# Batched 64x64 matrix products on one core: the first quarter of the first `a` tile loaded as three transfers of 32, 32 and 64 partitions

## The chip, the cores and the metric

The kernel runs on one core of one Trainium2 chip. A core has a matrix engine (TensorE, PE), VectorE (DVE), ScalarE (ACT), GpSimd (POOL) and SyncE (SP), and sixteen DMA engines which move data between the chip's main memory and the core's own. Each of SyncE, ScalarE and GpSimd can issue transfers, and each of them has a DMA queue of its own. The metric is the device time of one execution in microseconds.

## The reference

```python
def setup_inputs():
    return {
        "a": np.random.randn(1024, 64, 64).astype(np.float32),
        "b": np.random.randn(1024, 64, 64).astype(np.float32),
    }

def reference(a, b):
    return np.matmul(a, b).astype(np.float32)
```

There are 1024 independent products of a 64x64 matrix with a 64x64 matrix, with float32 in and out. Each of the three arrays has 16.8 MB. The kernel multiplies in bf16.

## The kernel before

The 1024 products are cut into 8 pairs of tiles (`s`, 128 products each), and into 16 tiles (`t`, 64 products each). For each `s`, one tile of `a` and one of `b` are loaded, 128 partitions wide, in four quarters (`h`, 32 products each).

**Loads.** Most loads are issued by GpSimd (`load_a`, L83, and `load_pair`, L113): each brings 32 partitions, 512 KB of float32 from main memory, and turns them into 256 KB of bf16 on the way. They go four to an `a` or `b` tile. The first `a` tile alone takes another path (`load_first_a`, L85 to L96): it is loaded as float32, with no conversion, by SyncE (quarters 0 and 2) and ScalarE (quarters 1 and 3), each quarter in one transfer of 128 partitions with 4 KB each, 512 KB in all. In this path a product's 64 rows lie in four partitions with 16 rows each, so a quarter's 32 products fill 128 partitions. The view that is read is this one, where `g` counts the products of a quarter and `mp` the four row blocks of a product:

```python
a_v = a.rearrange("(s g h) (mp v) k -> s h g mp (v k)", h=4, g=32, v=16)
```

The quarters land in two buffers that later serve as output tiles (`o_sb`), two quarters to a buffer.

**Turning the first tile.** `turn_first_a(h)` runs for h = 0 to 3 in this order. It turns quarter h into bf16 (L103: VectorE for h = 0, ScalarE for h = 1, 2 and 3) and transposes it in blocks of 32x32 on VectorE (L104). Each cast waits for the whole of its quarter.

**Spreading, products, evacuation.** `spread` (L142 for the first two tiles, L149 later) copies the transposed `a` into block-diagonal tiles `at_bd`, which are zeroed once (L252 on VectorE, L253 and L257 on GpSimd). `turn` (L121) and `turn_a` (L129) transpose `b` and the later `a` tiles on VectorE. `products` (L195) multiplies on TensorE, and `evacuate` (L207, L213) copies the results from PSUM to an output tile, mostly on ScalarE. `store(t)` sends the output tile out in two halves of 512 KB (L222).

**Order.** The order on each engine is written out by hand at the end of the kernel (L248 to L287). On GpSimd it is: a memset (L253), the four loads of `b` for s = 0, four of `a` for s = 1, four of `b` for s = 1, a memset (L257), `a` and `b` for s = 2, and from then on the stores with the loads of later tiles between them. GpSimd's transfers use eight semaphores in turn, so the ninth is issued only after the first has landed: eight are in flight at most. The four stores of the last tile are in pieces of 256 KB, three on SyncE and one on ScalarE. SyncE has nothing else in its queue than its two quarters of the first `a` tile and these three stores.

Of the kernel before, what the change touches and what calls it, by code (L numbers as in the profile page):

```python
# [12 lines left out]
def kernel(  # L13
# [14 lines left out]
    nc = tc.nc  # L28
# [19 lines left out]
    }  # L48
    LAST_QUEUE = {0: nc.sync, 2: nc.sync, 4: nc.scalar, 6: nc.sync}

    a_v = a.rearrange("(s g h) (mp v) k -> s h g mp (v k)", h=4, g=32, v=16)
    ap_v = a.rearrange("(s g h) m k -> s h g (m k)", h=4, g=32)
    bp_v = b.rearrange("(s g h) k n -> s h g (k n)", h=4, g=32)
# [31 lines left out]
    def load_first_a():  # L85

        raw = [
            o_pool.tile([128, 8, 4, 64], fp32, name="o_sb")[:].rearrange(
                "p gh w n -> p (gh w n)"
            )  # L90
            for _ in range(2)
        ]
        parts = [raw[h % 2][:, 1024 * (h // 2) : 1024 * (h // 2) + 1024] for h in range(4)]
        for h in range(4):
            (nc.scalar if h % 2 else nc.sync).dma_start(out=parts[h], in_=a_v[0, h])
        a_tiles[0] = parts  # L96

    def turn_first_a(h):
# [148 lines left out]

    with tc.manual_schedule():  # L248
        load_first_a()
        nc.vector.memset(warm[:, 0:1], 0.0)  # L250
        nc.scalar.copy(warm[:, 1:2], warm[:, 0:1])  # L251
# [66 lines left out]
```

## Time and profile before

| | us |
|---|---|
| median of 3 runs | 128.21 (127.74 to 128.29) |
| the profiled execution | 128.62 |
| its span, from the first to the last instruction | 126.8 |
| VectorE busy | 102.9 (81%) |
| ScalarE busy | 96.0 (76%) |
| GpSimd busy | 64.9 (51%) |
| TensorE matmuls busy | 54.9 (43%) |
| SyncE's two issues of the first `a` tile | 0.58 and 0.63 |
| issue to landing, SyncE's quarters, median | 5.8 |
| issue to landing, ScalarE's quarters, median | 7.4 |
| issue to landing, GpSimd's loads, median | 9.5 |

The profile shows one execution. Its engines' lines give busy times; in its slices a digit is the busy share of a fortieth of the span in tenths. The DMA lines tell how busy the sixteen DMA engines were and what they moved, counted as written. In the views by time, the first number is the start in microseconds from the beginning of the span and the second the duration; after the instruction, square brackets hold the idle time of the engine before it and what ended that idle time. The letter q behind an engine (SPq) marks its sequencer, which issues transfers.

### The profile page before, as it was taken

The page shows a single profiled execution, that of the slowest core. Times are in us where ns is not written, and L with a number is a line of the kernel's source. Part 1 is how long each engine was busy: PE and PEld are TensorE (multiplying, and loading weights), DVE is VectorE, ACT ScalarE, POOL GpSimd, SP SyncE. Part 2 cuts the span into 40 slices and gives each one's busy share as a digit, 9 for nine tenths or more (in the row PEclk, how much of TensorE's full clock was granted, in tenths as well). Part 3 has the DMA queues.
Part 4 walks back from the last instruction along what each step waited for, and adds up shares of the span by engine and source line. Part 5 has one row for each costly group of instructions (what it writes and reads, how often), then busy time and mean ns, then how long its engine had stood idle before and what let it go on. Part 6 is the DMA issues. An engine that isn't in the chain of part 4 may idle for free.

```text
span 126.8 us, 2680 instructions
## 1 busy us (share of the span) xinstructions
PE 54.9 (43%) x1088; PEld 51.7 (41%) x1088; DVE 102.9 (81%) x93; ACT 96.0 (76%) x151; POOL 64.9 (51%) x96
## 2 busy tenths in 40 slices
PE   0000019028645485847352942047510777079400
PEld 0000019028645484847352932046510776079300
DVE  4956999999999999999969696896949789780810
ACT  2157920399999999999999889918898299999700
POOL 8962797428544655625544446474554464333100
PEclk9999999955586555555955599657755555555965
DMA  2999999999999999999999999999999999999992
GB/s 59 392 327 209 212 217 217 212 215 207 264 293 257 264 290 292 291 292 278 265 275 290 291 288 284 275 275 275 296 288 283 275 273 279 383 406 396 343 342 99
DMA packets 8875, 34.76 MB, mean 274 GB/s; under 512 B 1568, under 2 KB 2592, under 8 KB 6944
## 3 DMA queue, kind: packets, MB, share of 16 engines
q0 software_dynamic: 7200, 31.46, 91.9%
q1 hardware_dynamic: 1104, 1.84, 4.3%
q10 hardware_dynamic: 560, 1.31, 2.7%
q8 instruction: 8, 0.13, 0.4%
q14 instruction: 3, 0.02, 0.0%
HBM read 33.55 MB, written 16.78 MB: 397 GB/s over the span
## 4 chain that ended last, share of the span: by engine, by line
DMA 57%; DVE 15%; ACT 7%; issue 7%; PE 5%; POOL 3%; ACTq 1%; DVEq 0%; POOLq 0%
DMA a_sb<-in_a_dram 28%; DMA b_sb<-in_b_dram 15%; DMA out_dram<-o_sb 7%; DMA o_sb<-in_a_dram 7%; DVE at_sb L129 6%; ACT o_sb L213 4%; PE o_ps L195 3%; DVE b_bf L121 3%; POOL out_dram L222 3%; ACT at_bd L149 2%; DVE o_sb L213 2%; DVE at_bd L142 2%; PE t_ps L195 1%; DVE at_bd L149 1%; ACT a_bf L103 1%
## 5 line engine op out<-in xcount | busy, mean ns | idle before, releaser
L195 PE MATMUL o_ps<-b_bf,at_bd 128*128 128x64 bf16 (+1 forms) x1024 | 52.0, 232 | 63.7 <-ACT o_sb L213 35.7
L195 PEld LDWEIGHTS <-at_bd 128*128 128x128 bf16 (+1 forms) x1088 | 51.7, 127 | 66.8 <-issue 43.0
L213 ACT COPY o_sb<-o_ps 64x512 f32<-64x512 f32 x112 | 65.0, 580 | 7.7 <-PE o_ps L195 6.1
L222 POOL DMA_DIRECT2D out_dram<-o_sb x30 | 23.8, 792 | 31.1 <-DMA a_sb<-in_a_dram 8.4
L121 DVE STREAM_TRANSPOSE b_bf<-b_sb 128x1024 f32<-128x1024 f32 x16 | 34.3, 2195 | 4.9 <-DMA b_sb<-in_b_dram 4.7
L129 DVE STREAM_TRANSPOSE at_sb<-a_sb 128x1024 f32<-128x1024 f32 x14 | 26.2, 1948 | 3.8 <-issue 2.4
L149 DVE COPY at_bd<-at_sb 32x1024 f32<-32x1024 f32 x40 | 28.2, 705 | 1.1
L113 POOL DMA_DIRECT2D b_sb<-in_b_dram x32 | 17.7, 554 | 14.9 <-DMA b_sb<-in_b_dram 6.9
L149 ACT COPY at_bd<-at_sb 32x1024 f32<-32x1024 f32 x16 | 16.7, 1043 | 8.6 <-DVE at_sb L129 8.3
L83 POOL DMA_DIRECT2D a_sb<-in_a_dram x28 | 16.4, 590 | 6.3 <-DMA out_dram<-o_sb 4.7
L103 ACT CAST a_bf<-o_sb 128x1024 bf16<-128x1024 f32 x3 | 3.1, 1045 | 4.7 <-DMA o_sb<-in_a_dram 4.7
L213 DVE COPY o_sb<-t_ps 64x256 f32<-64x256 f32 x8 | 3.4, 422 | 3.9 <-PE t_ps L195 3.8
L104 DVE STREAM_TRANSPOSE at_sb<-a_bf 128x512 f32<-128x512 f32 x4 | 4.2, 1048 | 2.6 <-ACT a_bf L103 2.6
L142 ACT COPY at_bd<-at_sb 32x512 f32<-32x512 f32 x8 | 4.9, 615 | 0.2
L252 DVE MEMSET at_bd<- 128x4096 f32 x1 | 3.5, 3472 | 0.8 <-issue 0.8
L253 POOL MEMSET at_bd<- 128x4096 f32 x1 | 3.5, 3512 | 0.3 <-POOLq L302 0.3
L257 POOL MEMSET at_bd<- 128x4096 f32 x1 | 3.5, 3537 | 0.0
L142 DVE COPY at_bd<-at_sb 32x512 f32<-32x512 f32 x8 | 3.3, 414 | 0.2
L251 ACT ACT_TABLE_LOAD x1 | 1.3, 1283 | 2.3 <-issue 2.3
L195 PE MATMUL t_ps<-b_bf,at_bd 128*128 128x64 bf16 x64 | 3.0, 224 | 0.0
L213 ACT COPY o_sb<-t_ps 64x256 f32<-64x256 f32 x8 | 2.9, 367 | 0.1
L207 ACT COPY o_sb<-o_ps 128x1024 f32<-128x1024 f32 x2 | 1.9, 1015 | 0.1
(7 smaller groups left out, 1.4 us busy)
## 6 DMA issues: line engine op xcount, KB each, us to landing
out_dram<-o_sb POOLq DMA_DIRECT2D x30, 512.0 KB, 9.3
b_sb<-in_b_dram POOLq DMA_DIRECT2D x32, 256.0 KB, 9.5
a_sb<-in_a_dram POOLq DMA_DIRECT2D x28, 256.0 KB, 9.5
o_sb<-in_a_dram ACTq DMA_DIRECT2D x2, 512.0 KB, 7.4
o_sb<-in_a_dram SPq DMA_DIRECT2D x2, 512.0 KB, 5.8
out_dram<-o_sb SPq DMA_DIRECT2D x3, 256.0 KB, 5.4
out_dram<-o_sb ACTq DMA_DIRECT2D x1, 256.0 KB, 5.5
```

Of the source, the lines that this page charges most:

```text
L83: nc.gpsimd.dma_start(out=a_tiles[s][32 * h : 32 * h + 32], in_=ap_v[s, h])
L103: (nc.scalar.copy if h else nc.vector.tensor_copy)(rows, a_tiles[0][h])
L104: nc.vector.transpose(at_tiles[0][:, h].rearrange("p g w mp vo -> p w vo g mp"), rows.bitcast(fp32).rearrange("p (vo w kp) -> p w vo kp", ...
L113: nc.gpsimd.dma_start(out=b_tiles[s][32 * h : 32 * h + 32], in_=bp_v[s, h])
L121: nc.vector.transpose(cols[:, u], rows[:, u])
L129: nc.vector.transpose(cols[:, 2 * half : 2 * half + 2].rearrange("p mp vo w g -> p (mp vo) w g"), rows[:, 2 * half : 2 * half + 2].rearran ...
L142: copy(bd[rows, 8 * i : 8 * i + 8, :, h, :, :].rearrange("p g w mp vo -> p (g w) (mp vo)"), at_sb[block : block + 32, h].rearrange("p g w ...
L149: copy(bd[rows, :, :, h, :, :].rearrange("p g w mp vo -> p (g w) (mp vo)"), at_sb[rows, half].rearrange("p g w mp vo -> p (g w) (mp vo)"),)
L195: nc.tensor.matmul(place, at_bd[:, w, g, :, u], b_bf[:, g, 64 * u : 64 * u + 64], start=u == 0 and (first or not split), stop=u == 1 and ( ...
L213: copy(rows[64 * par : 64 * par + 64, :, :, wl, :], o_ps[64 * wl : 64 * wl + 64, :, par, :, :],)
L222: store_queue(t, lo).dma_start(out=o_v[t, :, lo : lo + n, :], in_=o_sb[:, lo : lo + n].rearrange("p gh w n -> p (gh w n)"),)
L252: nc.vector.memset(bd_tiles[0][:], 0.0)
```

## The change

Quarter 0 of the first `a` tile was one transfer on SyncE. It becomes three on SyncE: products 0 to 8, 8 to 16 and 16 to 32 of the quarter, that is 32, 32 and 64 partitions, with 128, 128 and 256 KB. The other three quarters stay as they are, on the same queues; SyncE's quarter 2 stands behind the three pieces in its queue. The cast of quarter 0 waits for all three. Nothing else in the program changes, on any engine, apart from the numbers of lines, which grow by nine.

```diff
+    FIRST_LOADS = [
+        (0, nc.sync, 0, 8),
+        (0, nc.sync, 8, 16),
+        (0, nc.sync, 16, 32),
+        (1, nc.scalar, 0, 32),
+        (2, nc.sync, 0, 32),
+        (3, nc.scalar, 0, 32),
+    ]
...
-        for h in range(4):
-            (nc.scalar if h % 2 else nc.sync).dma_start(out=parts[h], in_=a_v[0, h])
+        for h, queue, lo, hi in FIRST_LOADS:
+            queue.dma_start(out=parts[h][4 * lo : 4 * hi], in_=a_v[0, h, lo:hi])
         a_tiles[0] = parts
```

## The prediction

> **What bounds the kernel now.** I read the slices first, then the queues, then stretches of one and two microseconds, then the order of time around the first tile.
>
> ```profile
> DMA  2999999999999999999999999999999999999992
> GB/s 59 392 327 209 212 217 217 212 215 207 264 293 257 264 290 292 291 292 278 265 275 290 291 288 284 275 275 275 296 288 283 275 273 279 383 406 396 343 342 99
> DMA packets 8875, 34.76 MB, mean 274 GB/s; under 512 B 1568, under 2 KB 2592, under 8 KB 6944
> ...
> q0 software_dynamic: 7200, 31.46, 91.9%
> q1 hardware_dynamic: 1104, 1.84, 4.3%
> q10 hardware_dynamic: 560, 1.31, 2.7%
> ```
>
> The sixteen DMA engines are busy from the second slice (3.2 us long) to the last but one. The GB/s row changes only with the kind of transfer: GpSimd's loads turn float32 into bf16, so that 256 KB written are 512 KB read. Queue 0 is GpSimd's; queue 1 is SyncE's, with the two quarters of `a` that the change concerns. The same in stretches:
>
> ```profile
> 2.00:3.00 1.00, 0.00 (x0) 0.00 (x0) 1.00 (x1) 0.69 (x1) 1.00 (x1) 1.00 0.83 147
> ...
> 5.00:6.00 1.00, 0.00 (x0) 0.00 (x0) 0.96 (x3) 0.00 (x0) 1.00 (x3) 1.00 1.04 418
> ...
> 7.00:8.00 1.00, 0.00 (x0) 0.00 (x0) 0.57 (x1) 0.39 (x1) 1.00 (x3) 1.00 1.30 459
> 8.00:9.00 1.00, 0.00 (x0) 0.00 (x0) 0.47 (x1) 0.33 (x1) 0.42 (x1) 1.00 0.94 197
> ...
> 33.00:34.00 1.00, 1.00 (x23) 1.00 (x21) 1.00 (x1) 0.99 (x2) 0.20 (x1) 0.50 1.00 385
> ...
> 122.00:124.00 2.00, 0.00 (x0) 0.00 (x0) 0.00 (x0) 0.00 (x0) 0.00 (x0) 0.50 1.03 346
> 124.00:126.80 2.80, 0.00 (x0) 0.00 (x0) 0.00 (x0) 0.00 (x0) 0.00 (x0) 0.50 0.18 62
> ```
>
> The last two numbers are DMA share and GB/s (packets count where they start, so a share may pass 1). Data flow from a little after 2 us; until 8 us it is the first `a` tile at 410 to 460 GB/s, then the rate halves: GpSimd's converting loads, the first issued at 4.19, have taken over. From 3 to 124 us there is no gap. So what the change does to an engine of arithmetic costs nothing unless it starves the DMA engines; what it does to their work or its split counts in full.
>
> ```profile
> 0.73 1.54 ACTq L95 DMA_DIRECT2D o_sb<-in_a_dram  x2
> ...
> 0.74 1.26 SPq L95 DMA_DIRECT2D o_sb<-in_a_dram  x2
> ...
> 5.09 0.79 DVE L103 CAST a_bf<-o_sb 128x1024 bf16<-128x1024 f32 x1
> ...
> 8.67 1.04 ACT L103 CAST a_bf<-o_sb 128x1024 bf16<-128x1024 f32 x1 [1.28 <-DMA o_sb<-in_a_dram]
> ...
> 10.56 1.05 ACT L103 CAST a_bf<-o_sb 128x1024 bf16<-128x1024 f32 x1 [0.84 <-DMA o_sb<-in_a_dram]
> ...
> 27.85 0.79 POOL L222 DMA_DIRECT2D out_dram<-o_sb  x1 [2.92 <-ACT o_sb L213]
> ...
> 33.80 0.79 POOL L222 DMA_DIRECT2D out_dram<-o_sb  x1 [1.08 <-DMA b_sb<-in_b_dram]
> ```
>
> SyncE issues two quarters in 1.26 us. The first has landed when VectorE leaves its memset at 5.09, the third (SyncE's second) at 8.65, the fourth (ScalarE's second) at 10.54. The first store waits for arithmetic that began with that landing. By 33.80 GpSimd is held by transfers again: it may have eight in flight.
>
> **The change part by part.** *Issues.* SyncE's two issues take 583 and 627 ns; there will be four, so the third quarter is issued at 2.55 instead of 1.37, 1.2 us later. Nothing else stands in SyncE's queue until the last stores at 118 us, so the two issues cost nothing themselves. The trace has no issue of 32 partitions; the nearest rows are these and the final stores' 373 to 489 ns, which bound the delay at 0.75 to 1.25 us. I take 1.2.
>
> *First quarter.* Its last piece is issued 1.2 us later, so it lands near 6.3 instead of 5.07. VectorE's cast and transpose (0.79 and 1.06) then end at 8.2 and the second quarter's transpose at 9.2, while before it waited 0.45, 1.28 and 0.84 us among the four transposes and began the third at 9.75. Nothing; without that idle time it would be 1.2 us of VectorE.
>
> *Bytes.* The 512 KB are the same, in rows of 4 KB as before. Two more transfers bring at most 32 more completion packets among 8875: nothing.
>
> *Split over the engines.* The page has 1568 packets under 512 B: 16 for each of its 98 transfers. Each of those transfers has an outermost size of 32 or 128, which sixteen divides; the new ones read 8, 8 and 16 rows of four matrix blocks. Eight rows cannot be dealt row by row to sixteen engines. If eight engines take the first two pieces, each carries 4 + 4 + 4 packets of 4 KB for this quarter and the other eight carry 4, where each carried 8. A packet takes 0.16 us (4 KB at 410 GB/s divided by 16), so half the engines are 4 x 0.16 = 0.64 us later and half 0.64 us earlier, and nothing later evens it out, for the rest is dealt equally and there is no gap. The bounds are 0 (dealt evenly) and +0.64, and -0.64 if the engines that end last are those relieved. I take +0.64, because a wait is for all sixteen parts and the later half decides it.
>
> The Trainium skill (DMA: Bandwidth & Descriptors, section "Why a DMA increments its semaphore by 16 and not by 1") says that a transfer uses the largest number of engines up to 16 that divides the slowest dimension on both sides, and on SyncE's queue the lowest-numbered ones. By it the pieces run on 8, 8 and 16 engines and the sum gains 0.64; by the rows, where every transfer has sixteen parts, 0. No run here shows it.
>
> *Landing of the third quarter.* The loaded engines have 36 packets of the first tile instead of 32, the last four of them when GpSimd's loads flow. Each then costs between 0.16 (queues drained one by one) and 0.16 + 0.62 (one software packet between two; 256 KB at 212 GB/s are 1.2 us for two packets on each engine): 0.6 to 3.1 us. The third quarter then lands last and ScalarE, which casts in order, casts the fourth behind it: up to 1.05 more. So VectorE's spreading, transposes and the first store are 0.6 to 4.1 us late; I take the middle, 2.3.
>
> *Cover of that delay.* GpSimd stood still from 24.93 to 27.85 with eight loads queued. They last until about 32.8 (from 33 the rate is a store's, 385). A GpSimd transfer needs up to 3.5 us from issue to flow, by the first: issued at 4.19, flowing at 7.7. Spare: 32.8 - 27.85 - 3.5 = 1.45 us. A delay of 2.3 leaves a gap of 0.85; the loaded engines are 0.64 behind anyway and see 0.2 of it. Bounds: 0 to 2.6.
>
> **Sum:** 0.64 + 0.2 = +0.84 us. The profiled execution took 128.62 (span 126.8 and 1.8 around it), 0.41 above the median of 128.21; a difference carries over, and I forecast 129.46 for an execution like that one, **129.05** for the median.
>
> **The rivals.** *Nothing moves (128.2).* The pieces are dealt to sixteen engines and the DMA engines stay full. For it: every 32-partition load in the trace ends in sixteen parts, and the delay of a quarter, 1.2 us, is below the spare 1.45. Against: the outermost 8. In this case the change does not do what it says to the first data either: they cannot flow earlier, for the first issue stands at 0.74 as before.
>
> *The first store starves the queue (130.8).* The worst end of the delay, 4.1 us: the store at 31.95, flowing at 35.45, 2.6 us after the loads ran out. It decides from a delay of 1.45 us on. For it: the fourth quarter already lands 1.9 us behind the third amid GpSimd's loads. Against: 3.5 us is a first transfer's figure, others may flow sooner.
>
> *The late engines are relieved (127.6).* The last 2.8 us have a share of 0.18, half a microsecond of full work: some engines end about a microsecond before the last. If the last ones are among those that lose four packets, their loads land, and the end comes, up to 0.64 us sooner: 127.57. It decides where the loaded half had over 0.64 us in hand. Against: it needs the late ones all in that half, and the first store in time.
>
> **How the numbers follow.** Forecast 0.42 (its own range 128.5 to 129.6), nothing moves 0.25, starved 0.15, relieved 0.18. A difference of 0.5%, 0.64 us, is about what a measurement of this kernel can tell from none. Faster (below 127.57): 0.15, most of the last case. Same: 0.25, with 0.08 of the forecast and 0.03 of the relieved, 0.36. Slower (above 128.85): the rest of the forecast, 0.34, and starved, 0.15, 0.49. The range runs from 127.5, the whole relief, to 130.3, where half of the starved case lies outside.
>
> **What would show it.** Queue 1 counts 1120 packets if the pieces ran on 8, 8 and 16 engines, 1136 if each had sixteen parts. SyncE's issues: four, ending near 3.2. ScalarE's last L103 cast (here renumbered) begins at 11.2 to 14.7 instead of 10.56. GpSimd's first store is issued 0.6 to 4.1 us after 27.85, and the DMA share between 30 and 36 us shows a gap or none. I am wrong if the share stays full, all loads land as before and the time still moves by over 0.64 us, or if the third quarter lands before 9.

## The result: 6% slower, and the profile after

The changed kernel takes 135.64 us (median of 6 runs, 135.00 to 136.42), the kernel before 128.08 beside it (127.74 to 128.29): a ratio of 1.060, 95% interval 1.055 to 1.064. The profiled execution took 135.59 with a span of 133.7, 6.9 us more than before. Ratios here are of runs within 1.5% of the fastest of their kernel, which leaves out, among others, nine of the 41 runs of the kernel before, eight of them at 131.4 to 132.9 us; no trace of these was kept, so whether they are the clash described below stays open. The slices of the changed kernel, and its SyncE queue:

```profile
DMA  3999999999099999999999999999999999999891
GB/s 71 369 265 207 213 213 208 221 206 211 12 223 237 212 275 282 297 286 286 283 278 284 267 281 281 283 293 283 292 282 273 282 273 286 370 404 382 324 342 64
DMA packets 8891, 34.76 MB, mean 260 GB/s; under 512 B 1584, under 2 KB 2608, under 8 KB 6960
...
q1 hardware_dynamic: 1120, 1.84, 4.4%
```

The eleventh slice is new: the DMA engines, busy without a break before, move 12 GB/s there. The same hole by the microsecond (the last two numbers are DMA share and GB/s):

```profile
33.00:34.00 1.00, 0.00 (x0) 0.00 (x0) 0.99 (x2) 0.97 (x2) 0.00 (x0) 0.89 0.57 115
34.00:35.00 1.00, 0.00 (x0) 0.00 (x0) 0.97 (x2) 0.98 (x3) 0.00 (x0) 0.50 0.04 8
35.00:36.00 1.00, 0.57 (x12) 0.57 (x12) 1.00 (x1) 0.96 (x3) 0.33 (x1) 0.50 0.00 0
36.00:37.00 1.00, 1.00 (x24) 1.00 (x21) 1.00 (x2) 0.99 (x2) 1.00 (x3) 0.50 0.00 0
37.00:38.00 1.00, 0.48 (x11) 0.37 (x9) 1.00 (x1) 0.96 (x3) 0.45 (x1) 0.50 1.00 344
```

The shares of the first four lines leave 0.43 + 0.96 + 1 + 1 = 3.4 us idle. What leads there, in order of time:

```profile
0.74 2.92 SPq L104 DMA_DIRECT2D o_sb<-in_a_dram  x4
...
9.31 0.69 DVE L112 CAST a_bf<-o_sb 128x1024 bf16<-128x1024 f32 x1 [4.14 <-DMA o_sb<-in_a_dram]
...
14.14 1.99 ACT L112 CAST a_bf<-o_sb 128x1024 bf16<-128x1024 f32 x2 [8.12 <-DMA o_sb<-in_a_dram]
...
15.22 2.00 DVE L113 STREAM_TRANSPOSE at_sb<-a_bf 128x512 f32<-128x512 f32 x2 [3.29 <-ACT a_bf L112]
...
16.97 3.53 POOL L266 MEMSET at_bd<- 128x4096 f32 x1
17.08 5.05 DVE L151 COPY at_bd<-at_sb 32x512 f32<-32x512 f32 x4
...
35.67 0.79 POOL L231 DMA_DIRECT2D out_dram<-o_sb  x1 [9.26 <-ACT o_sb L222]
```

SyncE's third quarter (issued last of its four) lands at 14.12; before, the last quarter had landed at 10.54. ScalarE then casts two quarters in a row, and VectorE's last transpose of the first tile ends at 17.22 instead of 12.69: 4.53 us late. VectorE's four copies into the block-diagonal tile then begin 0.11 us behind GpSimd's memset of another such tile, and take 5.05 us instead of 1.71: 3.34 us more. Together 7.87, and the first store is issued 7.82 us later, at 35.67 instead of 27.85. By then the loads queued ahead of it have run out. The four copies as the line's own view shows them, first of the changed kernel, then of the kernel before (shortest, middle and longest in ns):

```profile
L151 DVE COPY at_bd<-at_sb x8: 414/418/3700, 17.1 to 27.7; 32x512 f32<-32x512 f32 x8
```

```profile
L142 DVE COPY at_bd<-at_sb x8: 385/416/424, 12.5 to 19.9; 32x512 f32<-32x512 f32 x8
```

One copy of the eight takes 3.70 us, and it ends 0.3 us after the memset. In the kernel before, the same two instructions stood in this order of time:

```profile
12.54 1.71 DVE L142 COPY at_bd<-at_sb 32x512 f32<-32x512 f32 x4
...
14.94 3.54 POOL L257 MEMSET at_bd<- 128x4096 f32 x1
```

The four copies were done at 14.25; the memset began 0.69 us behind them and lay over transposes. In the changed kernel the memset is 2.0 us later too, for the four loads ahead of it wait for landings, but the copies are 4.5 us later.

Of the 6.9 us of span, 3.4 are the hole. Some 1.1 had been lost ahead of it: by the completion records, the middle one of the sixteen parts of GpSimd's sixteenth load landed at 29.23 instead of 28.10. Of the other 2.4, about 1.7 come in the next nine transfers, while the queue fills again: the middle part of the first store lands 4.55 us later than before, that of the thirtieth transfer 6.22. The rest is not split further.

### The profile page after: what moved, and what is told of

Its sections match the earlier page's. It is cut to its first block, busy times and chain, and to the rows that moved or that the text cites. A ratio compares the mean times of both kernels' runs of the same rounds, so it can differ in the third digit from the quotient of the medians.

```text
span 133.7 us, 2685 instructions
## 1 busy us (share of the span) xinstructions
PE 53.5 (40%) x1088; PEld 50.3 (38%) x1088; DVE 105.3 (79%) x93; ACT 95.9 (72%) x151; POOL 62.7 (47%) x96
## 3 DMA queue, kind: packets, MB, share of 16 engines
q1 hardware_dynamic: 1120, 1.84, 4.4%
## 4 chain that ended last, share of the span: by engine, by line
DMA 35%; ACT 28%; DVE 15%; issue 8%; POOL 5%; PE 4%; DVEq 0%; ACTq 0%; POOLq 0%
ACT o_sb L222 21%; DMA a_sb<-in_a_dram 20%; DMA b_sb<-in_b_dram 8%; DMA out_dram<-o_sb 7%; ACT at_bd L158 6%; DVE at_sb L138 6%; DVE at_bd L151 5%; PE o_ps L204 3%; POOL at_bd L262 3%; DVE o_sb L222 2%; DVE b_bf L130 2%; POOL b_sb L122 1%; POOL out_dram L231 1%; DVE at_bd L158 1%; PE t_ps L204 1%
## 5 line engine op out<-in xcount | busy, mean ns | idle before, releaser
L204 PEld LDWEIGHTS <-at_bd 128*128 128x128 bf16 (+1 forms) x1088 | 50.3, 126 | 74.2 <-issue 43.0
L158 DVE COPY at_bd<-at_sb 32x1024 f32<-32x1024 f32 x40 | 27.6, 690 | 1.1
L122 POOL DMA_DIRECT2D b_sb<-in_b_dram x32 | 16.4, 513 | 18.0 <-DMA b_sb<-in_b_dram 9.7
L92 POOL DMA_DIRECT2D a_sb<-in_a_dram x28 | 15.5, 557 | 6.4 <-DMA out_dram<-o_sb 4.8
L151 DVE COPY at_bd<-at_sb 32x512 f32<-32x512 f32 x8 | 6.6, 831 | 0.2
L112 DVE CAST a_bf<-o_sb 128x1024 bf16<-128x1024 f32 x1 | 0.7, 694 | 4.1 <-DMA o_sb<-in_a_dram 4.1
L204 PE MATMUL t_ps<-b_bf,at_bd 128*128 128x64 bf16 x64 | 2.0, 193 | 0.0
```

The costliest lines, as they stand in the source:

```text
L92: nc.gpsimd.dma_start(out=a_tiles[s][32 * h : 32 * h + 32], in_=ap_v[s, h])
L112: (nc.scalar.copy if h else nc.vector.tensor_copy)(rows, a_tiles[0][h])
L122: nc.gpsimd.dma_start(out=b_tiles[s][32 * h : 32 * h + 32], in_=bp_v[s, h])
L151: copy(bd[rows, 8 * i : 8 * i + 8, :, h, :, :].rearrange("p g w mp vo -> p (g w) (mp vo)"), at_sb[block : block + 32, h].rearrange("p g w ...
L158: copy(bd[rows, :, :, h, :, :].rearrange("p g w mp vo -> p (g w) (mp vo)"), at_sb[rows, half].rearrange("p g w mp vo -> p (g w) (mp vo)"),)
L204: nc.tensor.matmul(place, at_bd[:, w, g, :, u], b_bf[:, g, 64 * u : 64 * u + 64], start=u == 0 and (first or not split), stop=u == 1 and ( ...
```

## The experiments

The theory after the result (S): the first store comes too late for the DMA engines, which never make up an idle microsecond. Two causes of its lateness were to be told apart: the uneven split over the DMA engines (U) against the additional issues ahead of the third quarter (I). And a third, VectorE's copy that waits for GpSimd's memset (L).

**Two transfers of 64 partitions.**

```diff
-        (0, nc.sync, 0, 8),
-        (0, nc.sync, 8, 16),
+        (0, nc.sync, 0, 16),
         (0, nc.sync, 16, 32),
```

> Quarter 0 in two transfers of 64 partitions on SyncE: 16 rows outermost, so sixteen engines can take each, and one more issue instead of two. Theory U (the uneven split of the 32-partition pieces made the third quarter late): landings as before, third quarter by 9, first store near 28, time 128 to 128.6. Rival I (the additional issues ahead of the third quarter on SyncE made it late, 1.2 us of the start of the delay): half the additional issues, so the third quarter lands near 12 to 13 and the time is 130 to 132.

Measured: 132.29, 132.36, 135.04 and 135.36 us, a ratio of 1.032 (1.030 to 1.035). The trace is of the execution of 135.04: in it the third quarter landed at 13.31, the four copies took 5.42 us beside the memset, and the first store was issued at 35.22. U alone is refuted: sixteen rows outermost do not save the kernel.

**Three pieces of the same sizes, cut along the columns,** each with 128 partitions:

```diff
+        (0, nc.sync, 0, 256),
+        (0, nc.sync, 256, 512),
+        (0, nc.sync, 512, 1024),
...
+            queue.dma_start(out=parts[h][:, lo:hi], in_=a_v[0, h, :, :, lo:hi])
```

> Quarter 0 in three transfers of 128, 128 and 256 KB as in the changed kernel, but cut along the columns, so that each has 128 partitions and an outermost 32; its rows are 1, 1 and 2 KB instead of 4. Theory U: queue 1 has 1104 + 32 completion packets + 640 more data packets, third quarter lands by 9.5, time 128 to 129. Rival I: SyncE's third quarter is issued as late as in the changed kernel, lands near 14, first store near 35, time 134 to 136.

Measured: 133.63 us, ratio 1.039 (1.030 to 1.047). Third quarter at 12.12, copies 5.11 us beside the memset, first store at 33.70. Between the two numbers expected, nearer to I: most of the loss comes without an uneven split. What is missing to 135.64 is the split's part, or two microseconds of the landing; this run does not tell them apart.

**More loads ahead of the first store,** in the changed kernel:

```diff
-        0: ("a", 3),
...
         load_pair(2)
+        load_a(3)
```

> The changed kernel with the four loads of a for s = 3 issued by GpSimd ahead of the first store instead of between its halves. Theory S (the DMA engines run dry because the first store is issued at 35.7 and no load is queued behind those of s = 2): four loads more are 4 x 1.24 = 5 us of cover, the stretch from 33.5 to 37 is filled, first store still near 35.7, time 130.5 to 132. Rival W (the late arithmetic itself sets the end, as ScalarE is busy without a gap from 33 to 66): time unchanged, 135 to 136.

Measured: 132.59 us, 1.033 (1.029 to 1.037). The first store is as late as before it, 36.08, and yet 3 us came back, a little less than expected; no slice is empty. So ScalarE's late arithmetic is not what sets the end. The rest was not regained. The middle part of the 16th GpSimd transfer was already 2.3 us late, and from the 26th to the 28th transfer the delay grows from 2.0 to 3.7; I put this down to the stores, now issued one behind the other without loads between, but no run isolates it.

**The memset elsewhere,** in the changed kernel:

```diff
         load_a(1)
+        nc.gpsimd.memset(bd_tiles[2][:], 0.0)
         load_pair(1)
-        nc.gpsimd.memset(bd_tiles[2][:], 0.0)
```

> The changed kernel with GpSimd's second memset (at_bd 2) moved from behind the loads of b for s = 1 to ahead of them, where GpSimd waited 4.3 us. Theory L (VectorE's copy of 3.70 us at 17.08 waits for that memset, which runs until 20.50): the four copies take 1.7 us instead of 5.05, first store near 32.3, the gap in the DMA engines shrinks by 3.3 us, time 131.8 to 133. Rival (the copy is long for another reason, or the gap is not what costs): first store stays within 1 us of 35.7, time 135 to 136.

Measured: 131.74 us, 1.027 (1.024 to 1.030).

```profile
16.48 1.71 DVE L151 COPY at_bd<-at_sb 32x512 f32<-32x512 f32 x4
...
31.76 0.79 POOL L231 DMA_DIRECT2D out_dram<-o_sb  x1 [5.28 <-ACT o_sb L222]
```

The four copies take 1.71 us, the first store is issued at 31.76, and the time falls by 3.9 us, a little more than expected. L holds. The hole is gone (no slice of the DMA row between the first and the last is below 9), and the kernel is still 2.7% slower: the middle part of GpSimd's 16th transfer is 2.0 us later than in the kernel before, ahead of the first store, and this delay stays to the end. The moved memset lay over VectorE's cast of quarter 0, which took 3.42 us instead of 0.69; VectorE had to wait for the third quarter anyway.

**The issues alone:** the kernel before, quarter 0 whole, with two small transfers behind it on SyncE.

```diff
+        pad = consts.tile([16, 256], fp32)
...
+            if h == 0:
+                for i in (0, 128):
+                    nc.sync.dma_start(out=pad[:, i : i + 128], in_=ap_v[0, 0, 0:16, i : i + 128])
```

> The kernel before, quarter 0 whole, with two small transfers (16 partitions of 512 B each, dealt to sixteen engines) on SyncE between quarter 0 and quarter 2: the additional issues alone. Theory I (issued 1.2 us later, SyncE's second quarter lands last, amid GpSimd's loads, near 12; VectorE's four copies then begin after GpSimd's memset and take 5 us instead of 1.7): first store near 33.5, time 130.5 to 132.5. Theory U (only the uneven split or the cutting of quarter 0 is to blame): last quarter by 10.6, first store by 28.5, time 128 to 128.6.

Measured: 132.15 us; one of the four runs took 128.70 and the other three 132.00 to 132.69, the profiled one, 132.29, among these. In order of time:

```profile
10.87 1.99 ACT L107 CAST a_bf<-o_sb 128x1024 bf16<-128x1024 f32 x2 [3.42 <-DMA o_sb<-in_a_dram]
...
13.79 5.31 DVE L146 COPY at_bd<-at_sb 32x512 f32<-32x512 f32 x4
...
14.84 3.53 POOL L261 MEMSET at_bd<- 128x4096 f32 x1
...
32.64 0.79 POOL L226 DMA_DIRECT2D out_dram<-o_sb  x1 [7.88 <-ACT o_sb L217]
```

The third quarter lands at 10.84, only 0.3 us after the last one of before, but now it is the last, and ScalarE casts the fourth behind it. The copies begin 1.25 us late, two of them get in ahead of the memset, the third takes 4.00 us, until 0.3 us behind it, and the first store is 4.8 us late. Three runs against one are too few for a ratio; the argument rests on this order of time and on the next run.

**The same with the memset out of the way.** The edit is that of the memset run.

> The kernel with two small transfers between SyncE's quarters, and GpSimd's second memset ahead of the loads of b for s = 1, where it ends before VectorE's copies begin. If the memset is what turns 1.2 us of late transposes into 4.8 of a late store: four copies in 1.7 us, first store near 29.2, time 128.2 to 129.2, in every run. If the issues cost by themselves: 131 to 132.5 as without the move.

Measured: 128.68 us in 10 runs, 1.006 (1.002 to 1.009).

```profile
8.70 3.54 POOL L260 MEMSET at_bd<- 128x4096 f32 x1
9.60 1.99 ACT L107 CAST a_bf<-o_sb 128x1024 bf16<-128x1024 f32 x2 [2.46 <-DMA o_sb<-in_a_dram]
...
12.54 1.77 DVE L146 COPY at_bd<-at_sb 32x512 f32<-32x512 f32 x4
...
27.89 0.79 POOL L226 DMA_DIRECT2D out_dram<-o_sb  x1 [3.72 <-ACT o_sb L217]
```

Four copies in 1.77 us, and the first store where it was before. But here the third quarter also landed sooner, at 9.58, so that the copies were not late at all: the landing varies by more than a microsecond from execution to execution. In the kernel before and the three runs below that leave its loads of the first tile as they were, the last quarter landed between 8.75 and 11.34. With the memset away no run was longer than 130.14, and eight of the ten lie in the range expected. The issues and the moved memset together cost 0.6% (0.9% at most by the interval); the kernel before with the memset alone moved was not run. That the memset turns a delay of one microsecond into one of nearly five is read from the trace without the move (1.25 us late, and copies of 5.31 us instead of 1.71) and from the memset run above, not from this trace.

**The column pieces with the memset out of the way.**

> The run with three column pieces (even over the engines), with GpSimd's second memset moved ahead of the loads of b for s = 1. If the late landing and the memset together starve the queue: without the memset in the way the four copies take 1.7 us, the first store is issued near 30.4, before the loads of s = 2 run out at 32.8, no gap, time 128.2 to 129.2. If the split costs by itself: 131 and more.

Measured: 130.53 us, 1.013 (1.010 to 1.017), above the range. The first store is issued at 31.18, not 30.4, because the moved memset held VectorE's cast of quarter 0 for 4.63 us, until 12.35. So a first store 3.3 us late was already too late, though the DMA engines stood idle for only 0.2 us between 32 and 38 us.

**A late first store alone:** the kernel before, with seven idle copies on ScalarE.

```diff
+        pad = consts.tile([128, 1024], bf16)
+        for _ in range(7):
+            nc.scalar.copy(pad[:], a_tiles["first"][:, 0])
```

> The kernel before with seven idle copies of 1.04 us on ScalarE ahead of its first evacuation, nothing else changed: the first store alone is late, by 7.3 us, near 35.2, while the loads of the first tile are as before. Theory S (a first store after 32.8 - 1.3 = 31.5 leaves the DMA engines dry, and they never make it up): a gap of 3.7 us and some more at the second store, time 132 to 133.5. Rival (the lost time comes from the first 14 us): time 128 to 129.

Measured: 134.49 us (133.35 to 138.53), 1.041 (1.033 to 1.050), at the upper end of the range or above it. In order of time, and by the microsecond:

```profile
24.47 7.51 ACT L271 COPY pad<-a_bf 128x1024 bf16<-128x1024 bf16 x7
...
34.63 0.79 POOL L222 DMA_DIRECT2D out_dram<-o_sb  x1 [10.42 <-ACT o_sb L213]
```

```profile
32.00:33.00 1.00, 0.00 (x0) 0.00 (x0) 1.00 (x1) 0.99 (x2) 0.00 (x0) 0.50 0.26 49
33.00:34.00 1.00, 0.00 (x0) 0.00 (x0) 1.00 (x2) 0.98 (x3) 0.00 (x0) 0.50 0.00 0
34.00:35.00 1.00, 0.61 (x12) 0.60 (x12) 1.00 (x1) 0.96 (x3) 0.36 (x1) 0.50 0.00 0
35.00:36.00 1.00, 1.00 (x23) 1.00 (x21) 0.47 (x1) 0.99 (x2) 1.00 (x3) 0.50 0.01 4
```

Nothing about the first tile's transfers is changed here, and the hole is much the same: 3.7 us idle, and 5 us lost in the end. S holds, and the lateness of the first store suffices for most of the loss. ScalarE's later work is late here too, as in the changed kernel; the run with more loads ahead of the first store speaks against that as the cause.

**The clash alone:** the kernel before, with the memset three loads earlier.

```diff
-        load_pair(1)
+        load_pair(1, range(0, 1))
         nc.gpsimd.memset(bd_tiles[2][:], 0.0)
+        load_pair(1, range(1, 4))
```

> The kernel before with GpSimd's second memset moved up by three loads, so that it runs from about 11.7 to 15.3, over VectorE's four copies of 12.54. Theory L: one copy waits for its end, first store 2.5 to 3.2 us later, near 30.7; theory S says that this is still in time (the limit is 31.5), so the time is 128 to 128.8. Rival (every delay of the first store counts in full): 130.5 to 131.5.

Measured: 129.30 us in 10 runs, 1.006 (1.003 to 1.009).

```profile
11.81 3.53 POOL L257 MEMSET at_bd<- 128x4096 f32 x1
...
13.36 3.61 DVE L142 COPY at_bd<-at_sb 32x512 f32<-32x512 f32 x4
...
30.51 0.79 POOL L222 DMA_DIRECT2D out_dram<-o_sb  x1 [5.82 <-ACT o_sb L213]
```

The memset stands ahead of the copies, one copy waits until it ends, and the first store is 2.66 us late, 0.8 us of it because the last quarter landed 0.8 us later in this execution. By the ratio that costs 0.8 us: between the two expectations. The limit is not at 31.5, and it is not sharp. Nor is the loss idle time alone: between 32 and 38 us the DMA engines show none here. In this run and in the column run with the memset moved, the middle part of the 16th transfer is 0.1 and 0.15 us later than before, that of the 26th 1.4 and 1.9, and so it stays to the end. What holds the transfers up around the first store no run shows.

**Both mends together,** memset behind the loads of `a` for s = 2, loads of `a` for s = 3 ahead of the first store: in the changed kernel, in the one with column pieces, and (with the memset ahead of the loads of `b` for s = 1) in the kernel before.

> The changed kernel with both mends: GpSimd's second memset behind the loads of a for s = 2 (over VectorE's transposes, not its copies) and the loads of a for s = 3 ahead of the first store. First store near 32.5 with loads queued until about 38. What is left is the price of the uneven split on the DMA engines: 128.7 to 130.2 if the loaded half stays 0.6 to 2 us behind, 128.0 to 128.5 if it costs nothing.

> The run with three column pieces, dealt evenly, with the same two mends. First store near 30.5, loads queued until about 37. The cut itself should cost nothing then: 127.9 to 128.7. The difference to the run with the uneven pieces and the same mends is what the uneven split costs.

> The kernel before with the memset moved ahead of the loads of b for s = 1 and the loads of a for s = 3 ahead of the first store. The DMA engines had no gap in it, so nothing is to be won: 127.7 to 128.5, first store 27.2 to 28. If small gaps after 33 us cost something in the kernel before, 127.0 to 127.6.

Measured: 131.33 us (1.027, 1.024 to 1.029), 130.29 (1.017, 1.010 to 1.024) and 129.22 (1.011, 1.003 to 1.020), all three above what was expected. The mends are not free: in the first two the memset now lay over the copies of the second tile (3.31 and 4.65 us instead of 1.73), so that the first store came at 34.32 and 33.09; and in the kernel before the first store, behind four more loads, came at 30.09 instead of 27.2 to 28, without a gain. They serve as a pair: by the ratios the uneven pieces are 1.0% (1.2 us) behind the column pieces with the same mends, and 1.4% (1.7 us) with the memset alone moved. The kernels of a pair differ in the size of their rows and in the first store as well, so this is not the price of the uneven split alone. None of the kernels tried beats the kernel before.

Where the loads ahead of the first store are the same as before, its issue goes with the span of the same execution:

| kernel | first store, us | span, us |
|---|---|---|
| before | 27.85 | 126.8 |
| issues, memset moved | 27.89 | 126.9 |
| clash alone | 30.51 | 127.5 |
| columns, memset moved | 31.18 | 128.7 |
| changed, memset moved | 31.76 | 129.6 |
| issues alone | 32.64 | 130.5 |
| columns | 33.70 | 131.7 |
| late store alone | 34.63 | 131.5 |
| two of 64 partitions | 35.22 | 133.3 |
| changed | 35.67 | 133.7 |

From 30.5 on, a microsecond of the first store goes with 1.2 of span ((133.7 - 127.5) / (35.67 - 30.51)); without the kernels cut along the partitions, with 1.0 ((131.5 - 127.5) / (34.63 - 30.51)). The first two or so cost little. The rows of the kernels cut along the partitions also hold the 1 to 2 us by which their loads were late before the first store.

## Why the prediction was wrong

The direction and the mechanism were among the cases: a late third quarter, a late first store, DMA engines without work. The size was not.

*The step that failed* is "Landing of the third quarter", where its delay was carried to the first store as it stood, 0.6 to 4.1 us, 2.3 taken. Two things are wrong in it. First, the landing was put down to four more packets on the loaded engines, 0.6 to 3.1 us, and to nothing else. Against its own landing before (8.65) the third quarter came 5.47 us late, at 14.12, and the transposes, which had waited for the fourth quarter until 10.54, came 4.53 us late, a little beyond the upper end. The later issue, which the prediction put at nothing, has a part in it: with the additional issues alone the quarter landed at 10.84 and 9.58, with the column pieces at 12.12, 10.79 and 11.99, with the uneven pieces, in four traces, at 13.52 to 14.52. Second, the copies behind the transposes were taken at their old duration. The margin was in the trace: copies done at 14.25, GpSimd's memset at 14.94. The copies came 4.5 us later and the memset 2.0, and under it the copies took another 3.34 us. Neither the sum nor a rival had this step; the prediction looked at VectorE's queue and not at what GpSimd would be doing at the new time. The Trainium skill has the rule (SBUF — State Buffer, section "Who interferes with whom"): a VectorE copy in a fast mode that uses two ports and a GpSimd instruction lock each other out for a whole instruction, whoever comes second waits, while VectorE instructions with one input outside these modes are not affected. The runs agree: 0.42 us against 3.70 for a copy, and transposes of 2.1 us beside a memset as elsewhere. Who comes second cannot always be told from the times: the cast of 4.63 us in the column run began 0.50 us ahead of the memset, while GpSimd was issuing transfers, and waited all the same.

*Cover.* The spare time was put at 1.45 us, and the table above says about 2. The number was near, but not for the reasons given: a store flows 1.4 us after its issue (35.67 to 37.03), not 3.5, while a late store costs time before the loads run out. With the measured delay the prediction's own rule gives a gap of 7.82 - 1.45 = 6.4 us; the gap was 3.4. That the span grew by 6.9 is no support for the rule, but luck. So the rival of the starved queue was right in kind and had its chance (0.15) and its price (2.6 us) too low by the missing step.

*Split over the engines.* Right in kind. Queue 1 counts 1120 packets, the number named for 8, 8 and 16 engines, as the cited rule of the Trainium skill (DMA: Bandwidth & Descriptors) says; each of the first two pieces has eight parts that land (4.81 to 5.53 and 6.72 to 7.88); and the third quarter's sixteen parts land in two groups, one by 9.97 and one from 11.25 on. Priced at 0.64 us, the pieces cost more. GpSimd's 16th transfer, ahead of the first store, lands 1.1 to 1.6 us later than before on the mean of its parts in the four traces with the uneven pieces, and up to 1.8 to 2.6 us later when the parts are taken in order of landing; with the column pieces the mean is 0.1 to 0.7, with the issues alone 0.0. How much of this is the uneven split is open. In the trace of two pieces of 64 partitions all sixteen parts are late alike, by 1.2 to 2.0 us. The prediction put the bytes at nothing, but the packets of the first tile kept the sixteen engines busy for 5.6 to 6.0 us with the loads of the kernel before, 6.0 to 6.3 with column pieces, 6.7 to 6.9 with the uneven pieces and 7.4 with two of 64 partitions. So cutting along the partitions may cost by itself. This rival no run separates from the split.

*Issues and first quarter.* The third quarter was issued 1.7 us later rather than 1.2 (four issues of 591 to 877 ns), and this delay was not carried to its landing. Quarter 0 landed at 9.18, not 6.3, and VectorE waited 4.14 us for it; this cost nothing, as said, but only because the third quarter was later still.

*Nothing moves, and relieved.* Both wrong: the DMA engines did not stay full, and no gain came from the lighter half.

## What to carry to other kernels

This kernel, which keeps the DMA engines full, lost little from late arithmetic until the first store, which stands in order behind it, was some two microseconds late; from there on every microsecond counted. So before a change that delays the head of a chain, look along the chain, at its new time, for an instruction of another engine that it will run beside, and for the margin to it in the trace. And a first transfer cut into pieces moves everything behind it in its queue: check what the new last landing feeds. Whether cutting the last transfer of a queue is safer was not tried.

## What the runs showed of the hardware that I had not expected

Pieces with fewer partitions lost the race for the DMA engines: with quarter 0 whole or in pieces of 128 partitions SyncE's data flowed first, at 2.13 to 2.17 us, and with first pieces of 32 or 64 partitions ScalarE's whole quarter did, at 2.13 to 2.16, and SyncE's only from 3.8 to 4.2 on, though both queues issue at 0.74. What orders the two queues no run shows. And a late first store goes with slower loads around it: a packet of a converting load took 685 ns on average between 28 and 50 us in the changed kernel, 641 in the kernel before, and 626 and 625 in both later. Idle time is not needed for it: it was 667 in the clash run and 675 in the column run with the memset moved, where the DMA engines stood idle for 0.2 us at most. What makes the packets slower no run shows.
